# Converting DMAs on GpSimd's queue write the rounded part of the mixers' weight slabs

## The chip, the cores and the metric

One core of a Trainium2 chip runs the whole program. The metric is the device time of one execution in microseconds (us). The engines are TensorE (PE; its weight loads are listed as PEld), VectorE (DVE), ScalarE (ACT), GpSimd (POOL) and SyncE (SP); SyncE does nothing here but issue DMAs. TensorE's clock has two levels, 1.2 and 2.4 GHz; the granted clock is the share of the higher one that the profile recorded.

## The reference

One inference step of a small two-layer backbone, for 128 context tokens and 256 latent tokens with the same weights. D_MODEL is 1024, D_FF 2816. Each layer is a half-step feed-forward, a mixer and a second half-step feed-forward:

```python
h = rmsnorm(x, g[0]) * (1.0 + mod[:, 1]) + mod[:, 0]
x = x + 0.5 * mod[:, 2] * swiglu(h, p["w_ffn_in"][0], p["w_ffn_out"][0])
h = rmsnorm(x, g[1]) * (1.0 + mod[:, 4]) + mod[:, 3]
m, new_ctx = mixer(h, p, lidx, ctx)
x = x + mod[:, 5] * m
```

and the second feed-forward as the first. The factors mod come from a conditioning vector through w_ada (1024 x 9216 in each layer). In the mixer one projection w_in (1024 x 2144) feeds three groups of heads: differential attention (queries, keys and values, 256 columns each), a bidirectional gated recurrence of width 512 (input and gate branch, 512 columns each) and latent attention (352 columns). Their outputs are concatenated and go through w_out (1024 x 1024). Everything is float32.

## The kernel before

Activations stand with features on the 128 partitions and the 384 tokens along the free axis (context first). All 384 tokens go through one pass of the weights, and each weight is read from HBM once, in slabs: `wslab` (L460 to L472) loads up to four blocks of 128 input rows by 256 output columns (512 KB) into a tile wx with one or two DMAs on SyncE's queue.

To keep float32 accuracy from the faster float32r matmuls, both operands are split into a rounded part and a remainder. For a slab ScalarE casts wx into wh (float32r, L470), and VectorE writes wl = wx - wh (L471). `mm3` (L474 to L477) then runs three matmuls per pair of blocks: wh with the high part of the activations, wh with their low part, and wl with the high part. The tiles wh have four buffers (tag H), the tiles wl four (tag L), the tiles wx five (tag X); all slabs of the kernel, those of the feed-forwards too, go through these buffers.

There are 332 slabs. The mixer of a layer has 30: 18 of w_in (key "in": two each for the two halves of the recurrence's input, two each for the two halves of its gate branch, two for the values of the differential attention, four of 352 columns by two blocks for the latent attention, two each for queries and keys) and 12 of w_out (key "out"; for each pair of output blocks one slab of four blocks and two slabs of two). In the profile the mixer's matmuls write psw (recurrence), psva (values), psc (latent attention, 352 columns), psa (queries, keys) and po (out projection). The recurrence itself is gates (psg, L891), activations on ScalarE with several table loads, and scans on VectorE (L923, L924); after each scan GpSimd copies one column into state_out (L926), eight times per mixer in two groups of four. After psc, ScalarE squares it and writes the normalised cl (L143), which TensorE transposes (pst, L989).

The order of instructions on each engine is fixed when the program is built: the Tile framework reckons when each instruction is ready and gives the engine the ready one of highest priority. `ahead(key)` raises the priority of what stands in it; "in" has an offset of 120, "out" none. On each engine the instructions then run in that order, and one that waits holds all behind it.

GpSimd's queue carries the loads of w_ada in both layers (adax, L354, three buffers), small parameter loads (L226, L770), four stores of new context tensors per layer, and the copies into state_out. The ada steps run in the feed-forwards and, 14 of them, in the attention of layer 0's mixer.

Of the kernel before, what the change touches and what calls it, by code (L numbers as in the profile page):

```python
# [18 lines left out]
P = 128  # L19
# [65 lines left out]
def hybrid_step_kernel(  # L85
# [40 lines left out]
    nc = tc.nc  # L126
# [28 lines left out]
    def ahead(key):  # L155
        return tc.high_priority(offset=AHEAD[key]) if key in AHEAD else nullcontext()
# [303 lines left out]
    def wslab(pieces, nk, ncol, key):  # L460

        shape = [P, HALF_K, 256] if ncol <= 256 else [P, HALF_K // 2, 512]
        x = wp.tile(shape, F32, name="wx", tag="X")
        for src, off in pieces:
            n = src.shape[1]
            nc.sync.dma_start(x[:, 0:nk, off : off + n], src.rearrange("(k p) n -> p k n", p=P))
        h = wp.tile(shape, F32R, name="wh", tag="H", bufs=4)
        lo = wp.tile(shape, F32R, name="wl", tag="L", bufs=4)
        with ahead(key):
            nc.scalar.copy(h[:, 0:nk, 0:ncol], x[:, 0:nk, 0:ncol])  # L470
            V.tensor_tensor(lo[:, 0:nk, 0:ncol], x[:, 0:nk, 0:ncol], h[:, 0:nk, 0:ncol].bitcast(F32), ALU.subtract)  # L471
        return h, lo  # L472

# [81 lines left out]
    def ffn_slab(s, f, q):  # L555
        win = w_ffn_in[s // 3, (s % 3) // 2]
        rows = slice(q * HALF_K * P, (q + 1) * HALF_K * P)
        return wslab(
            [(win[rows, f * P : (f + 1) * P], 0), (win[rows, DFF + f * P : DFF + (f + 1) * P], P)], HALF_K, 256, "fin"
        )  # L560

    def ffn(s, r, hs, last, ready=None):
# [42 lines left out]
        for m in range(0, KD, 2):  # L605
            p2 = [PS("po0", "pw"), PS("po1", "pw")]
            parts = [(k0, min(HALF_K, KF - k0)) for k0 in range(0, KF, HALF_K)]
            if m == KD - 2:
                parts = parts[-1:] + parts[:-1]
            for n_, (k0, nk) in enumerate(parts):  # L610
                h, lo = wslab([(wout[k0 * P : (k0 + nk) * P, m * P : (m + 2) * P], 0)], nk, 256, "fout")
                n = ADA_F[s][1]
                ada.step(min(n, n * (slot + 1) // 16) - min(n, n * slot // 16), True)
                slot += 1
                for j in range(2):
                    for kk in range(nk):
                        w0 = slice(j * P, (j + 1) * P)
                        mm3(
                            p2[j][:, 0:T],
                            h[:, kk, w0],  # L620
                            lo[:, kk, w0],
                            *acts[k0 + kk],
                            n_ == 0 and kk == 0,
                            n_ == len(parts) - 1 and kk == nk - 1,
                        )
            if m == 0 and not last:
                ada.until(s + 1, 1)
            if m == KD - 4 and s % 3 == 0:
                ada.finish()
                cache_prep(l)  # L630
            for j in range(2):
                residual(p2[j], m + j, s, last)
                if last:
                    store_y(m + j)
# [182 lines left out]
    def mixer(l, r_in, hs):  # L817
# [8 lines left out]
        def in_slabs(cols):  # L826
            ncol = sum(b - a for a, b in cols)
            out = []
            for q in range(2):
                pieces, off = [], 0  # L830
                for a, b in cols:
                    pieces.append((W[rows(q), a:b], off))
                    off += b - a
                out.append(wslab(pieces, HALF_K, ncol, "in"))
            return out
# [558 lines left out]
```

## Time and profile before

| what | us |
|---|---|
| median of 3 runs (1579.6 to 1581.04) | 1579.62 |
| the profiled execution's own time | 1580.6 |
| its span, first to last instruction | 1578.8 |
| TensorE busy | 1527.9 |
| VectorE busy | 1113.6 |
| ScalarE busy | 746.6 |
| GpSimd busy | 103.4 |

The profiled execution has 1.8 us around its span, and it stands 1.0 us above the median. Busy times are unions of the instructions' intervals. TensorE's matmuls overlap in its pipeline, so busy time there is not speed. A wait is put down to the semaphore that came last. The mixer of layer 0 lies from about 327 to 523 us of the span, that of layer 1 from about 1096 to 1290 us. The granted clock over the span is 0.991.

### The profile page before, as it was taken

What the parts mean: (1) busy time and instruction counts of PE and PEld (TensorE: products, weight loads), DVE (VectorE), ACT (ScalarE), POOL (GpSimd) and SP (SyncE); (2) the same over time, 40 slices, a digit from 0 to 9 for tenths busy, and PEclk for the clock granted to TensorE, in tenths of its full rate; (3) what the DMA queues carried; (4) which work ended last, traced back from release to release, by engine and by line L of the source; (5) the groups of instructions that cost most, each with busy time, mean ns of one, the idle gap of its engine ahead of it and who ended that gap; (6) DMA issues with size and microseconds to landing.
All of it is one profiled execution on the core that took longest, in us unless ns stands there. A gap on an engine that the chain in (4) does not pass through costs nothing.

```text
span 1578.8 us, 24260 instructions
## 1 busy us (share of the span) xinstructions
PE 1527.9 (97%) x9118; PEld 1441.2 (91%) x9118; DVE 1113.6 (71%) x2068; ACT 746.6 (47%) x1376; POOL 103.4 (7%) x194
## 2 busy tenths in 40 slices
PE   7999999999889999999999999999978999999998
PEld 5899999998668999999999999999857699999998
DVE  5888586587677988578578866777967789443332
ACT  4533332469577633333363333325975864333221
POOL 1202010001100001001000200110000000000000
PEclk9999999999999999999999999999989999999999
DMA  9978576523531587566537866674231046444341
GB/s 304 248 205 228 158 231 196 147 80 115 185 106 37 146 245 211 161 207 225 171 97 215 238 187 193 203 238 121 64 92 37 15 134 201 130 117 128 116 145 35
DMA packets 291034, 249.02 MB, mean 158 GB/s; under 512 B 11554, under 2 KB 273159, under 8 KB 290917
## 3 DMA queue, kind: packets, MB, share of 16 engines
q1 hardware_dynamic: 270224, 175.94, 38.2%
q0 software_dynamic: 20368, 71.34, 14.8%
q8 instruction: 71, 1.16, 0.3%
q14 instruction: 47, 0.38, 0.1%
q10 hardware_dynamic: 324, 0.20, 0.1%
HBM read 245.17 MB, written 2.27 MB: 157 GB/s over the span
## 4 chain that ended last, share of the span: by engine, by line
PE 88%; DVE 4%; ACT 4%; issue 2%; DMA 1%; POOL 0%; ACTq 0%; DVEq 0%; POOLq 0%
PE po L475 9%; PE po L476 9%; PE po L477 9%; PE pg L475 8%; PE pg L477 8%; PE pg L476 8%; PE pu L475 8%; PE pu L477 8%; PE pu L476 8%; PE psw L476 1%; PE psg L891 1%; PE psw L475 1%; PE psw L477 1%; PE adaps L378 1%; ACT gate L143 1%
## 5 line engine op out<-in xcount | busy, mean ns | idle before, releaser
L471 DVE TENSOR_TENSOR wl<-wx,wh 128x1024 fp32r<-128x1024 f32 (+2 forms) x332 | 385.4, 1163 | 302.8 <-ACT wh L470 294.3
L470 ACT CAST wh<-wx 128x1024 fp32r<-128x1024 f32 (+2 forms) x332 | 333.2, 1005 | 448.5 <-PE po L476 237.3
L362 DVE SCALAR_TENSOR_TENSOR ada<-adax,sc,ada 128x1024 f32<-128x1024 f32 x196 | 244.2, 1280 | 17.8 <-DMA adax<-in_w_ada_dram 17.4
L475 PE MATMUL po<-aH,wh 128*128 128x384 f32 x704 | 239.7, 341 | 0.0
L477 PE MATMUL po<-aH,wl 128*128 128x384 f32 x704 | 237.7, 338 | 0.0
L476 PE MATMUL po<-aL,wh 128*128 128x384 f32 x704 | 237.2, 337 | 0.0
L475 PE MATMUL pg<-hH,wh 128*128 128x384 f32 x640 | 216.9, 339 | 0.0
L475 PE MATMUL pu<-hH,wh 128*128 128x384 f32 x640 | 216.2, 338 | 0.0
L477 PE MATMUL pg<-hH,wl 128*128 128x384 f32 x640 | 215.9, 337 | 0.2 <-DVE wl L471 0.2
L477 PE MATMUL pu<-hH,wl 128*128 128x384 f32 x640 | 215.6, 337 | 0.0
L476 PE MATMUL pu<-hL,wh 128*128 128x384 f32 x640 | 215.5, 337 | 0.0
L476 PE MATMUL pg<-hL,wh 128*128 128x384 f32 x640 | 215.4, 337 | 0.0
L143 ACT ACTIVATE sg<-pg 128x384 f32<-128x384 f32 x80 | 39.4, 493 | 206.5 <-PE pg L477 206.5
L475 PEld LDWEIGHTS po<-aH,wh 128*128 128x128 f32 x704 | 132.4, 188 | 3.9 <-issue 2.1
L476 PEld LDWEIGHTS po<-aL,wh 128*128 128x128 f32 x704 | 132.2, 188 | 0.5 <-issue 0.5
L477 PEld LDWEIGHTS po<-aH,wl 128*128 128x128 f32 x704 | 132.2, 188 | 0.0
L354 POOL DMA_DIRECT2D adax<-in_w_ada_dram x128 | 68.1, 533 | 892.3 <-DVE ada L360 466.5
L475 PEld LDWEIGHTS pg<-hH,wh 128*128 128x128 f32 x640 | 120.2, 188 | 2.5 <-issue 2.1
L477 PEld LDWEIGHTS pg<-hH,wl 128*128 128x128 f32 x640 | 120.1, 188 | 0.6 <-DVE wl L471 0.5
L476 PEld LDWEIGHTS pg<-hL,wh 128*128 128x128 f32 x640 | 120.2, 188 | 0.0
L475 PEld LDWEIGHTS pu<-hH,wh 128*128 128x128 f32 x640 | 120.2, 188 | 0.0
L477 PEld LDWEIGHTS pu<-hH,wl 128*128 128x128 f32 x640 | 120.1, 188 | 0.0
(327 smaller groups left out, 2425.9 us busy)
## 6 DMA issues: line engine op xcount, KB each, us to landing
wx<-in_w_ffn_in_dram SPq DMA_DIRECT2D x352, 256.0 KB, 4.1
adax<-in_w_ada_dram POOLq DMA_DIRECT2D x128, 512.0 KB, 4.9
wx<-in_w_ffn_out_dram SPq DMA_DIRECT2D x80, 512.0 KB, 3.9
wx<-in_w_in_dram SPq DMA_DIRECT2D x28, 512.0 KB, 3.8
adax<-in_w_ada_dram SPq DMA_DIRECT2D x16, 512.0 KB, 7.7
wx<-in_w_ffn_out_dram SPq DMA_DIRECT2D x16, 256.0 KB, 3.3
wx<-in_w_out_dram SPq DMA_DIRECT2D x8, 512.0 KB, 3.9
wx<-in_w_out_dram SPq DMA_DIRECT2D x16, 256.0 KB, 2.7
```

Source lines behind the costliest of these rows:

```text
L143: ins = nc.scalar.activation(out, in_, func, **kw)
L354: nc.gpsimd.dma_start(x, w_ada[l, k * P : (k + 1) * P, c0 : c0 + D])
L362: ins = V.scalar_tensor_tensor(accs[c], x, w, accs[c], ALU.mult, ALU.add)
L378: mm(bank[32 * a : 32 * a + 32, 256 * c : 256 * c + 256], cm(C_ONE, n1=32), x[:, a], start=True, stop=True)
L470: nc.scalar.copy(h[:, 0:nk, 0:ncol], x[:, 0:nk, 0:ncol])
L471: V.tensor_tensor(lo[:, 0:nk, 0:ncol], x[:, 0:nk, 0:ncol], h[:, 0:nk, 0:ncol].bitcast(F32), ALU.subtract)
L475: mm(out, wh, xh, start=first, stop=False)
L476: mm(out, wh, xl, start=False, stop=False)
L477: last_mm[0] = mm(out, wl, xh, start=False, stop=last)
L891: mm(ps[:, 0:TG], wg[:, wi, :], xcs[ch], start=True, stop=True)
```

## The change

In the slabs with key "in" or "out" the rounded part wh is no longer cast by ScalarE from wx. Instead the same pieces of the weight are read from HBM a second time, by DMAs on GpSimd's queue whose destination is the float32r tile wh; the transfer converts. wx is still loaded by SyncE, and VectorE still subtracts wh from wx. The feed-forwards' slabs are as before. The DMA stands outside `ahead(key)`.

```diff
         h = wp.tile(shape, F32R, name="wh", tag="H", bufs=4)
         lo = wp.tile(shape, F32R, name="wl", tag="L", bufs=4)
+        if key in ("in", "out"):
+
+            for src, off in pieces:
+                n = src.shape[1]
+                nc.gpsimd.dma_start(h[:, 0:nk, off : off + n], src.rearrange("(k p) n -> p k n", p=P))
         with ahead(key):
-            nc.scalar.copy(h[:, 0:nk, 0:ncol], x[:, 0:nk, 0:ncol])
+            if key not in ("in", "out"):
+                nc.scalar.copy(h[:, 0:nk, 0:ncol], x[:, 0:nk, 0:ncol])
             V.tensor_tensor(lo[:, 0:nk, 0:ncol], x[:, 0:nk, 0:ncol], h[:, 0:nk, 0:ncol].bitcast(F32), ALU.subtract)
```

## Rows read from the trace of the kernel before

**Rows 1.** The page: busy time, share of the span, instructions.

```profile
PE 1527.9 (97%) x9118; PEld 1441.2 (91%) x9118; DVE 1113.6 (71%) x2068; ACT 746.6 (47%) x1376; POOL 103.4 (7%) x194
```

**Rows 2.** Busy time by stage, both mixers; the sum covers all eight stages.

```profile
core 0: us, PE busy (x) PEld busy (x) DVE busy (x) ACT busy (x) POOL busy (x), PEclk, DMA share, GB/s
327.00:400.00 73.00, 71.67 (x423) 61.70 (x421) 62.68 (x141) 66.14 (x129) 7.04 (x14) 1.00 0.33 100
...
503.00:523.00 20.00, 20.00 (x116) 20.00 (x116) 18.45 (x50) 12.68 (x25) 0.00 (x0) 1.00 0.57 164
...
sum 390.00, PE 358.00 PEld 302.39 DVE 311.52 ACT 289.80 POOL 21.39; mean PE 44.75 PEld 37.80 DVE 38.94 ACT 36.23 POOL 2.67
```

**Rows 3.** TensorE's waits, 327 to 440 us: total, times, longest.

```profile
PE psva L955 <- DVE wl L471: 0.6, 1, 0.6
PE psc L981 <- DVE wl L471: 0.4, 1, 0.4
```

**Rows 4.** TensorE's waits, 1096 to 1210 us.

```profile
PE pst L989 <- ACT cl L143: 6.5, 1, 6.5
...
PE psc L979 <- ACT wh L470: 1.4, 1, 1.4
PE psc L981 <- DVE wl L471: 0.8, 1, 0.8
```

**Rows 5.** ScalarE's casts by shape, whole span: busy, mean ns of one.

```profile
L470 ACT CAST wh<-wx 128x1024 fp32r<-128x1024 f32 x292 | 307.3, 1053 | 381.8 <-PE po L476 176.5 <-PE pu L476 148.9 <-DMA wx<-in_w_ffn_in_dram 38.0
...
L470 ACT CAST wh<-wx 128x512 fp32r<-128x512 f32 x32 | 19.9, 622 | 66.2 <-PE po L476 60.8 <-PE psa L1212 2.8 <-ACT rH L143 1.5
...
L470 ACT CAST wh<-wx 128x704 fp32r<-128x704 f32 x8 | 6.0, 779 | 0.5 <-PE psw L476 0.5
```

**Rows 6.** DMA issues: count, KB each, median us from issue to landing.

```profile
wx<-in_w_in_dram SPq DMA_DIRECT2D x28, 512.0 KB, 3.8
...
wx<-in_w_ffn_out_dram SPq DMA_DIRECT2D x16, 256.0 KB, 3.3
...
wx<-in_w_out_dram SPq DMA_DIRECT2D x16, 256.0 KB, 2.7
...
wg<-in_lru_w_gate_dram POOLq DMA_DIRECT2D x4, 256.0 KB, 7.7
...
ukv<-in_mla_w_ukv_dram POOLq DMA_DIRECT2D x2, 256.0 KB, 4.3
```

**Rows 7.** GpSimd in order of time, 260 to 400 us: start, us, what.

```profile
366.78 0.48 POOL L926 COPY state_out<-hscan 128x1 f32<-128x1 f32 x1 [89.25 <-DVE hscan L923]
...
369.56 0.43 POOL L926 COPY state_out<-hscan 128x1 f32<-128x1 f32 x1 [0.40 <-DVE hscan L923]
372.59 0.56 POOL L926 COPY state_out<-hscan 128x1 f32<-128x1 f32 x1 [2.60 <-DVE hscan L923]
...
388.38 0.53 POOL L354 DMA_DIRECT2D adax<-in_w_ada_dram  x1
389.76 0.56 POOL L926 COPY state_out<-hscan 128x1 f32<-128x1 f32 x1 [0.85 <-DVE hscan L923]
```

**Rows 8.** VectorE, 365 to 374 us: the second va slab's subtraction.

```profile
370.98 1.22 DVE L471 TENSOR_TENSOR wl<-wx,wh 128x1024 fp32r<-128x1024 f32 x1
```

**Rows 9.** ScalarE, 1150 to 1180 us: a cast between the squares of psc.

```profile
1166.79 1.06 ACT L470 CAST wh<-wx 128x1024 fp32r<-128x1024 f32 x1
```

**Rows 10.** ScalarE, 318 to 332 us: a cast that waits for its buffer.

```profile
322.72 1.05 ACT L470 CAST wh<-wx 128x1024 fp32r<-128x1024 f32 x1 [3.14 <-PE po L476]
```

**Rows 11.** VectorE, 318 to 332 us: the last residual, then a subtraction.

```profile
327.13 0.74 DVE L547 SCALAR_TENSOR_TENSOR xT<-po,md,xT 128x128 f32<-128x128 f32 x2
328.02 1.23 DVE L471 TENSOR_TENSOR wl<-wx,wh 128x1024 fp32r<-128x1024 f32 x1 [0.16 <-ACT wh L470]
```

**Rows 12.** The ada loads on GpSimd: ns least, median, most.

```profile
L354 POOL DMA_DIRECT2D adax<-in_w_ada_dram x128: 530/530/657, 2.5 to 1333.6; - x128
```

## The prediction

> **What bounds the kernel now.** I read the page's busy times first. TensorE is busy for 97% of the span and ScalarE for 47% [rows 1], so taking work from ScalarE can only pay where TensorE waits for ScalarE. The change touches the two mixers alone, so next come the stretches of the two mixers, measured with the table by stage: 327 to 523 us in layer 0, 1096 to 1290 us in layer 1. TensorE is busy there for 358.0 of 390.0 us [rows 2]; the 32 us of idle time are all that any relief of another engine could give back. In the first part of layer 0's mixer (input projections and the recurrence) ScalarE is the fullest engine beside TensorE, 66.14 of 73 us, yet TensorE is busy 71.67 us of them: the projections fill it while the recurrence runs on ScalarE and VectorE.
>
> Then TensorE's waits, by what ended them. In layer 0 those that name a weight slab are 0.6 us (the remainder wl at the va projection) and 0.4 us (wl at the psc projection) [rows 3]. In layer 1 the row of 0.6 us at va comes again, and at psc they are 0.8 us and, for the rounded part wh itself, 1.4 us; the longest wait there is 6.5 us for cl, the normalised psc, which comes from ScalarE [rows 4]. So slabs cost 3.8 us in both mixers together, and a chain in which ScalarE's casts stand costs 6.5 us more.
>
> **What is removed.** Each mixer has 30 slabs: 14 of 512 KB and 4 of 352 KB of w_in, 4 of 512 KB and 8 of 256 KB of w_out. Their casts last 1.05, 0.78 and 0.62 us by shape [rows 5], so 2 x (18 x 1.05 + 4 x 0.78 + 8 x 0.62) = 54 us leave ScalarE. Most of it lies beside TensorE's work and gives nothing. What I count is the chain to cl in layer 1, where one cast of 1.06 us stands among the squares of psc [rows 9] and a second of the same kind follows before the normalisation: 2.1 us. VectorE's own subtractions hold the same chain, so I take 1.5 us a mixer, **-3.0 us**; bounds 0 and -4.2 us (2.1 in each).
>
> **What is added, and its latency.** 60 DMAs with 26.0 MB, on GpSimd's queue. No row shows a converting DMA, nor one of this shape on that queue. SyncE's load of the same 512 KB lands after 3.8 us, 256 KB after 2.7 [rows 6]. For 256 KB GpSimd's ukv takes 4.3 us where SyncE's w_ffn_out load takes 3.3, so the queue adds 1.0 us: I take 4.8 us for 512 KB, 3.7 for 256 and, between them by size, 4.1 for 352 KB. From below it can't beat SyncE's 3.8; from above it is wg, 256 KB in short pieces, at 7.7 us; the pieces here are 1 KB as in SyncE's load, so I stay near that. The Trainium skill ("DMA: Bandwidth & Descriptors", Latency and other measured facts) puts the first byte at about 1 us on GpSimd's path against 0.6 us on SyncE's, so 0.4 us more, not 1.0; by it the sum below would be 1.2 us lower, and no row here separates first byte from the rest.
>
> The bytes are costed at nothing: the DMA engines are busy 0.33 of the first part and none of the waits in [rows 3, 4] names a wx load; even in the out projection of layer 0, busy 0.57 at 164 GB/s [rows 2], some 2.3 MB more in 22 us (105 GB/s) make 0.57 x 269 / 164 = 0.93 of them. If that cover were gone, landings would move towards the 7.7 us bound.
>
> **The issue slot.** A DMA leaves when its instruction reaches the head of GpSimd's queue and an H buffer is free. GpSimd waits in order, and in each recurrence eight copies into state_out stand on it, each waiting for a scan on VectorE. The framework orders each queue by when it reckons instructions ready: loads of ada weights that come later in the source stand between these copies [rows 7]. I place the new DMAs where the present casts and subtractions imply that their buffer was reckoned free: the second va slab about the third copy, the third psc slab about the sixth.
>
> Second va slab: the third copy starts at 369.56; a cast of 1.05 us ahead of it on ScalarE's chain is gone; 368.5 + 4.8 to land + 1.22 to subtract = 374.6, against an end of 372.2 now (370.98 + 1.22, [rows 8]): TensorE 2.4 us later. Third psc slab: the sixth copy at 389.76, less four casts gone (3.6), plus the 2.4 just added, plus 4.1 to land and 0.9 to subtract = 393.5; the wait of 0.4 us there ends at 393.0 now. That is less late than TensorE itself then is, so it adds nothing, and the late arrival takes up waits of today: 2.4 - 0.4 in layer 0, 2.4 - 1.4 in layer 1, **+3.0 us**. Bounds: the DMAs leave ahead of the copies and the 3.8 us of waits go (-3.8); or behind the fourth copy, 372.59 + 4.8 + 1.2 = 378.6, 6.4 late in each mixer (+12.8).
>
> **The wait that moves.** Today ScalarE stands at a cast until TensorE frees the buffer (3.14 us at 322.72, [rows 10]). That wait goes to GpSimd, where only other DMAs and copies stand behind it; but VectorE's subtraction then waits for a landing. Queued behind it on VectorE are the residual and the norm of the mixer's start, which TensorE needs at once. The buffer free at 322.7 lands at 327.5 and is subtracted by 328.7; the residual of the last chunk starts today at 327.13 [rows 11]. It may be 1.6 us late; as the subtraction can also be placed behind it, I take 1 us a mixer, **+2.0 us**. Bounds 0 and, for the next slab (subtracted from 328.02 on, [rows 11], so free one cast earlier, at 327.0; 4.8 + 1.2 later is 333.0 against 329.2 now), 3.8 each, +7.6.
>
> **Out projections: nothing.** TensorE runs 116 matmuls in 20 us [rows 2], 0.172 us each. With four H buffers, 48 matmuls (8.3 us) lie between the freeing of one and the use of its next slab; 4.8 + 1.2, or 3.7 + 0.7, fit. At 7.7 + 1.2 the 512 KB slabs would be 0.6 us late, at most +2 us in all.
>
> **Sum.** -3.0 + 3.0 + 2.0 = +2.0 us on the profiled execution's own 1580.6 (span 1578.8 and 1.8 around it). The median of the runs is 1579.6, 1.0 below it, so I predict **1581.6 us**: no change that a measurement of this kernel tells, for which I count 0.2%, 3.2 us either way. Against the median, all lower bounds give 1579.6 - 4.2 - 3.8 = 1571.6, with all upper ones 1579.6 + 12.8 + 7.6 + 2.0 = 1602.0.
>
> **Rivals.**
> *GpSimd's queue becomes the wait (slower).* The va slab's DMA stands behind the fourth state copy: +12.8 - 3.0 + 2.0 = +11.8, 1591 us. For it: GpSimd stands 89 us at the first copy [rows 7], and the present casts of these slabs come only after the square roots that feed the scans. Against: ada loads do slip between copies. It decides from the point where the second va slab's DMA is issued later than about 370 us. Chance 0.22.
> *VectorE stands at the subtractions (slower).* Each mixer's start pays the 3.8 us: -3.0 + 3.0 + 7.6, 1587 us. For it: VectorE waits for casts there today. Against: it has idle time just there. Chance 0.13.
> *The DMAs run ahead (faster).* They are issued as buffers come free, before the copies: -3.8 - 3.0, 1573 us; a subtraction is then never late. For it: the first slabs of each mixer do have an empty GpSimd queue (277 to 366 us, the 89 us before the first copy). Against: the later slabs do not. Chance 0.25.
> *VectorE holds up the descriptors (slower).* If an issue on GpSimd lasted until a VectorE instruction of a subtraction's length is over, four late slabs would be 1.22 us later each, +4.9 on the sum, 1586.5 us. Against it: 128 issues of ada loads beside a busy VectorE lasted 530 ns in the median and 657 at most [rows 12]. Chance 0.04. The Trainium skill ("SBUF — State Buffer", SBUF: two separate sides) warns of this: GpSimd can't write descriptors while VectorE runs an operation on both of its ports. By that rule this is where the time would go; the trace so far doesn't show it.
>
> **How the numbers follow.** Forecast 0.36; faster 0.25; slower 0.22 + 0.13 + 0.04 = 0.39. The slower cases together are as likely as the forecast, but each alone is less so. The forecast's own range is 1576.4 to 1582.8. Eight in ten: down to the run-ahead case (1573), up to a little above the queue case, 1594, since a landing of 7.7 us would lift all of them.
>
> **What would show it.** Right: state copies and wh DMAs interleaved on GpSimd; landings near 4.8 us; TensorE's waits naming wl or a wh DMA at psva and psc some 2 us longer, the wait for cl shorter. Wrong: landings above 7 us; wh DMAs issued after the fourth or eighth copy; adax waits of TensorE in layer 0 longer; or no wait for a slab at all and both mixers shorter.

## The result: slower by 1.0%

The changed kernel takes 1594.6 us (median of 4 runs, 1590.8 to 1599.3) against 1579.6 us before: ratio 1.0099, 95% interval 1.0080 to 1.0117. That is 15.0 us slower, just above the range of the prediction, whose forecast was no change. The profiled execution has a span of 1593.4 us, 14.6 more than that of before.

**Where the time went.** I cut each mixer at TensorE's first matmuls: the norm (psn), the va projection (psva), the end of psc, the query and key projection (psa), the first out projection (po), the next norm. Lengths in us, layer 0 / layer 1:

| stage | before | after | difference |
|---|---|---|---|
| start: norm, recurrence's projections | 43.0 / 43.0 | 49.1 / 45.9 | +6.1 / +2.9 |
| va and psc | 28.3 / 28.3 | 26.3 / 26.2 | -2.0 / -2.1 |
| cl, latent queries and keys | 20.0 / 19.6 | 20.9 / 21.5 | +0.9 / +1.9 |
| queries and keys, up to the first out projection | 28.4 / 26.9 | 30.4 / 29.9 | +2.0 / +3.0 |
| attention and the rest | 76.7 / 76.3 | 77.9 / 79.1 | +1.2 / +2.8 |
| mixer | 196.4 / 194.1 | 204.6 / 202.6 | +8.2 / +8.5 |

So 16.7 us are lost in the mixers. Ahead of the first mixer 3.5 us were won, where the profile of before has 6.8 us at half clock (at 43 us) and that of after none; behind the mixers 1.4 us were lost. The page's busy line of the changed kernel, against [rows 1], shows ScalarE 48 us less busy without its 54 us of casts and GpSimd 43 us busier, with TensorE's busy time hardly changed:

```profile
PE 1530.3 (96%) x9118; PEld 1442.1 (91%) x9118; DVE 1114.9 (70%) x2068; ACT 698.3 (44%) x1316; POOL 146.7 (9%) x254
```

Windows by these stages after the change, first layer 0, then layer 1, and in the last three lines of before: layer 0's sum, layer 1's last stage and its sum (columns as in [rows 2]: length, then busy time of each engine, TensorE's granted clock, DMA share, GB/s):

```profile
323.40:372.50 49.10, 44.62 (x219) 39.35 (x218) 39.88 (x99) 31.19 (x63) 7.00 (x11) 0.97 0.60 150
...
398.80:419.70 20.90, 13.94 (x87) 6.86 (x87) 13.75 (x33) 7.92 (x26) 5.96 (x11) 0.84 0.87 268
...
sum 204.60, PE 185.01 PEld 152.97 DVE 157.88 ACT 123.89 POOL 34.61; mean PE 37.00 PEld 30.59 DVE 31.58 ACT 24.78 POOL 6.92
...
1172.80:1194.30 21.50, 11.32 (x31) 6.41 (x31) 14.70 (x35) 7.97 (x26) 1.86 (x3) 0.71 0.52 140
...
1224.20:1303.30 79.10, 75.27 (x442) 64.42 (x443) 60.76 (x196) 50.48 (x149) 6.26 (x9) 0.92 0.33 85
sum 202.60, PE 179.83 PEld 153.97 DVE 155.45 ACT 124.44 POOL 25.75; mean PE 35.97 PEld 30.79 DVE 31.09 ACT 24.89 POOL 5.15
...
sum 196.40, PE 183.86 PEld 152.99 DVE 157.15 ACT 144.64 POOL 15.06; mean PE 36.77 PEld 30.60 DVE 31.43 ACT 28.93 POOL 3.01
...
1213.70:1290.00 76.30, 71.30 (x442) 61.04 (x443) 62.49 (x198) 55.66 (x157) 0.54 (x1) 0.98 0.20 60
sum 194.10, PE 174.64 PEld 149.90 DVE 154.87 ACT 145.28 POOL 6.34; mean PE 34.93 PEld 29.98 DVE 30.97 ACT 29.06 POOL 1.27
```

In layer 0 TensorE idles 204.6 - 185.0 = 19.6 us, in the same stages of before 12.5. In layer 1 it idles 22.8 against 19.5, and is busy 179.8 us against 174.6 for the same matmuls: there the granted clock is 0.92 in the last stage, where it was 0.98 before. So of the 16.7 us 10.4 are idle time (7.1 and 3.3) and 6.3 longer busy time. Over both mixers the records show 37.5 us at the lower of the two levels, before 20.5. Most of these stretches begin in or right after a wait of 2 us or more; two of 3.4 us (at 1243 and 1267 us) have only waits under 1 us ahead of them.

**TensorE's waits**, layer 0 (323 to 440 us), then layer 1 (1100 to 1225 us), against [rows 3, 4]:

```profile
PE adaps L368 <- DMA adax<-in_w_ada_dram: 6.4, 2, 6.1
PE psn L503 <- ACT sq L143: 3.3, 1, 3.3
PE psw L481 <- DMA wh<-in_w_in_dram: 1.2, 1, 1.2
...
PE psva L961 <- DVE wl L477: 0.4, 1, 0.4
...
PE pst L995 <- ACT cl L143: 8.2, 1, 8.2
PE po L481 <- issue: 3.3, 1, 3.3
```

The waits for slabs at psva and psc are smaller than before, not larger. What grew is the wait for the norm at the start (nothing before, 3.3 us now), for cl (6.5 before), for the first out projection (2.2 before) and, in layer 0, for an ada load (6.1 now, 3.7 before). The ada row of before is not among [rows 3]:

```profile
PE adaps L368 <- DMA adax<-in_w_ada_dram: 4.8, 2, 3.7
```

The new DMAs themselves show why the first of these waits grew. By line, their durations of issue in ns (least, median, most) and who waited for them (us, times):

```profile
  L473 POOL DMA_DIRECT2D wh<-in_w_in_dram x36: 696/740/1000, 310.5 to 1172.9; - x36
  L473 POOL DMA_DIRECT2D wh<-in_w_out_dram x24: 696/707/775, 429.7 to 1293.1; - x24
...
who waited for it (us, times):
  DVE wl L477: 17.2, 13
  PE psw L481: 1.2, 1
```

TensorE waited for a landing once; VectorE waited 13 times, 17.2 us in all, at subtractions. On VectorE at layer 0's start (time, length, and in brackets the idle time before) one sees what stands behind such a wait, against [rows 11]:

```profile
319.42 1.23 DVE L477 TENSOR_TENSOR wl<-wx,wh 128x1024 fp32r<-128x1024 f32 x1 [1.02 <-DMA wh<-in_w_in_dram]
...
326.12 1.23 DVE L477 TENSOR_TENSOR wl<-wx,wh 128x1024 fp32r<-128x1024 f32 x1 [3.40 <-DMA wh<-in_w_in_dram]
327.26 0.74 DVE L553 SCALAR_TENSOR_TENSOR xT<-po,md,xT 128x128 f32<-128x128 f32 x2
```

The second of these two subtractions waited for a DMA that GpSimd issued at 319.47, when TensorE freed the buffer:

```profile
319.47 0.74 POOL L473 DMA_DIRECT2D wh<-in_w_in_dram  x1 [3.45 <-PE po L482]
```

The residual of the feed-forward's last chunk begins 3.9 us after TensorE's norm began at 323.4 (before, 0.2 us: 327.13 against 326.9). The norm's last squares need it, and TensorE stands 3.3 us for them. Between the queries' projection and their norm, in layer 0, the same:

```profile
431.51 1.07 DVE L1179 TENSOR_REDUCE nst<-sq 128x8 f32<-128x256 f32 x3 [0.47 <-ACT sq L143]
...
433.92 1.22 DVE L477 TENSOR_TENSOR wl<-wx,wh 128x1024 fp32r<-128x1024 f32 x1 [1.13 <-DMA wh<-in_w_out_dram]
435.07 0.17 DVE L662 TENSOR_TENSOR nst<-nst 128x24 f32<-128x24 f32 x1
436.01 0.69 DVE L477 TENSOR_TENSOR wl<-wx,wh 128x512 fp32r<-128x512 f32 x1 [0.77 <-issue]
...
437.04 1.08 DVE L1185 TENSOR_TENSOR ya<-psa,nst 128x256 f32<-128x256 f32 x3
```

From the first reduction to the normalised ya it takes 5.5 us; before it took 3.2:

```profile
430.49 1.07 DVE L1173 TENSOR_REDUCE nst<-sq 128x8 f32<-128x256 f32 x3
...
433.69 1.09 DVE L1179 TENSOR_TENSOR ya<-psa,nst 128x256 f32<-128x256 f32 x3
```

The two subtractions are of w_out slabs that TensorE uses from 450.1 us on. A third place of this kind lies at the end of each mixer: VectorE stands 1.3 us (layer 0) and 0.65 us (layer 1) for the landing of the last w_out slab, with work of the next norm behind it, and TensorE waits 0.8 and 1.3 us at that norm. Before, and with w_out cast by ScalarE (e1 below), there is no such wait.

### The profile page after: what moved, and what is told of

The parts are those of the page before. It is cut to its first block, busy times and chain, and to the rows that moved or that the text cites. A ratio compares the mean times of both kernels' runs of the same rounds, so it can differ in the third digit from the quotient of the medians.

```text
span 1593.4 us, 24305 instructions
## 1 busy us (share of the span) xinstructions
PE 1530.3 (96%) x9118; PEld 1442.1 (91%) x9118; DVE 1114.9 (70%) x2068; ACT 698.3 (44%) x1316; POOL 146.7 (9%) x254
## 4 chain that ended last, share of the span: by engine, by line
PE 78%; issue 9%; DVE 5%; DMA 3%; ACT 3%; POOL 1%; SPq 0%; POOLq 0%; DVEq 0%; ACTq 0%
PE po L481 8%; PE po L482 8%; PE po L483 8%; PE pg L481 8%; PE pg L483 8%; PE pu L483 8%; PE pu L481 8%; PE pu L482 8%; PE pg L482 8%; DMA adax<-in_w_ada_dram 1%; DVE wl L477 1%; DMA wh<-in_w_in_dram 1%; PE adaps L378 1%; PE psO L1112 1%; PE psT L1085 1%
## 5 line engine op out<-in xcount | busy, mean ns | idle before, releaser
L476 ACT CAST wh<-wx 128x1024 fp32r<-128x1024 f32 (+1 forms) x272 | 278.9, 1025 | 420.4 <-PE po L482 207.3
L482 PEld LDWEIGHTS pu<-hL,wh 128*128 128x128 f32 x640 | 120.3, 188 | 0.0
```

The costliest lines, as they stand in the source:

```text
L482: mm(out, wh, xl, start=False, stop=False)
```

## The experiments

Each was timed against the kernel before on the same chip; ratios are to that kernel, with 95% intervals. Expected times take 1594.6 and 1579.6 us as the two ends.

**1. Which slabs cost.** The change for some slabs only; the others are cast by ScalarE as before. "in_xb" to "in_qk" name the slabs of w_in by their use: the recurrence's input (the start), its gate branch, va, psc, and queries and keys.

```diff
-        if key in ("in", "out"):
+        if key in ("in",):                                              # e1
+        if key in ("in_gb", "in_va", "in_c", "in_qk", "out"):           # e2
+        if key in ("in_gb", "in_va", "in_c"):                           # e3
```

> Only the slabs of w_in (14 of 512 KB and 4 of 352 KB a mixer) come by the converting DMA; the 12 slabs of w_out a mixer are cast by ScalarE as before. Theory 'VectorE stands at landings': the loss sits where VectorE, which works in order, waits for a landing with critical work behind it: at the mixer's start (6.1 us lost in layer 0, 2.9 in layer 1) and between the key projection and the scores (about 3 and 5.5 us lost), where the first slabs of w_out are subtracted. Only the second loss can go here, up to 8 us of it: about 1587 us. Rival 'queue and bytes': the cost is of the 26.0 MB on GpSimd's queue, 8 MB of them are gone, so about a third of the 15 us: 1590 us. Rival 'the out projections cost nothing and win nothing': 1594.6 us as with the whole change.

> The first four slabs of each mixer (the xb projections) are cast by ScalarE as before; the other 26 slabs come by the converting DMA. Theory 'VectorE stands at landings': the 6.1 and 2.9 us lost between the last FFN chunk and the first projections come back, 1585.5 us. If only the two norms' waits of TensorE (4.1 and 2.3 us with the change) come back, 1589. Rival 'queue and bytes': 4 MB of 26.0 gone, 1592.5 us. Rival 'the loss at the start is taken up later anyway': 1594.6 us.

> The converting DMA is kept where slabs are needed while ScalarE is fullest and VectorE's waits hold up nothing that is late (the gelu, va and psc projections, 10 slabs a mixer); the xb, query, key and out slabs are cast by ScalarE as before. Theory 'VectorE stands at landings': the losses at the start and around the attention are gone and the gain of the psc stage (2.0 and 1.7 us in the changed kernel) stays: about 1576 us, faster than before. Rival 'queue and bytes': 9.1 MB of the 26.0 remain, a third of the loss: about 1584.5 us. Rival 'the psc gain is taken up by the next wait': 1579.6 us, no change.

Measured: w_in alone 1588.3 us, 1.0058 (1.0038 to 1.0077); the start cast 1586.9 us, 1.0040 (1.0028 to 1.0052); the middle slabs alone 1579.7 us, 0.9996 (0.9987 to 1.0005). So the start costs 7.7 us (1594.6 - 1586.9), the w_out slabs 6.3 (1594.6 - 1588.3), the middle nothing. By the ratios it is some 9 and 6 us, with intervals of about 4 us either way. The second run rules out its rival of queue and bytes (1592.5); the first can't tell its theory (1587) from that rival (1590). The third expectation, 1576, was missed, and its rival 'taken up by the next wait' had the right time. By stages the start takes 43.1 us in both layers when it is cast, and the queries' stage 28.2 and 27.3 us when w_out is cast. The middle slabs keep the -2.4 us of their stage in each mixer, and the time is still that of before. In that profile TensorE idles 29.3 us in the mixers, 2.7 less than before, but 30.7 us of them are at the lower clock, before 20.5, and the mixers are 1.1 us longer: this relief of ScalarE is worth nothing in the end.

**2. Bytes and queue without anyone who waits.** ScalarE casts, and each mixer slab is also read by a converting DMA into a scratch tile that nothing reads; in the second kernel each waits for the cast of its slab, and in the third the query and key slabs have none.

```diff
+            d = wp.tile(shape, mybir.dt.bfloat16, name="wd", tag="HD", bufs=1)
...
+                twin = nc.gpsimd.dma_start(d[:, 0:nk, off : off + n], src.rearrange("(k p) n -> p k n", p=P))
+                tc.add_manual_dep(twin.ins, cast.ins.name, sync, reason="after the cast")   # e8, e15
```

> ScalarE casts every slab as before, and for every slab of the mixers GpSimd's queue also issues a converting DMA of the same source bytes into a scratch tile that nothing reads (bfloat16, for room, so the bytes written are half). Theory 'VectorE stands at landings': nothing waits for those landings, so the time is that of before, 1579.6 us, at most 3 us more for ada loads behind them. Rival 'queue and bytes': the loss is there without anyone waiting for a landing, 1588 to 1594 us.

> As the kernel with ScalarE's casts and a second, unread converting DMA of every mixer slab, but now each such DMA waits for the cast of its slab, so that the 60 DMAs fall where the slabs are used and not at the start of the program (the scratch is one bfloat16 buffer, so a DMA also waits for the one before it). Theory 'VectorE stands at landings': the queue and the source bytes alone cost little, 1580 to 1583 us. Rival 'queue and bytes': most of the loss is here, 1588 us or more.

> ScalarE's casts and the unread second DMA behind each cast, for 26 of the 30 slabs of a mixer: all but the query and key slabs, whose DMAs stood in front of ada loads on GpSimd's queue in layer 0. Theory 'the queue and the bytes cost only where an ada load that is due stands behind a slab': the time of before, 1579 to 1581 us. Rival 'bytes cost by themselves': the 8.8 us of the run with all 30 shrink only in proportion, to 1587 us.

Measured: 1689.3 us, 1.069 (1.0663 to 1.0717); 1588.8 us, 1.0063 (1.0047 to 1.0078); 1582.2 us, 1.0018 (1.0008 to 1.0027). The first says nothing on the question: its DMAs wait for no buffer of the mixers, so they ran from the start of the program, each waiting for the one before it at the single scratch buffer, with ada loads behind them on GpSimd's queue. VectorE stood 121.2 us for ada loads in the first 340 us (8.0 before), with the feed-forward's subtractions behind it, and the last pg matmul of the first feed-forward began at 334 us instead of 226. The second has the time that its rival named (1588 us or more), but all of the loss lies in one place of layer 0 (cl's stage, 31.0 us instead of 20.0), where GpSimd stood at the single scratch buffer with ada loads behind it:

```profile
400.49 0.78 POOL L477 DMA_DIRECT2D wd<-in_w_in_dram  x1 [7.09 <-DMA wd<-in_w_in_dram]
401.26 0.55 POOL L354 DMA_DIRECT2D adax<-in_w_ada_dram  x1
409.06 0.74 POOL L477 DMA_DIRECT2D wd<-in_w_in_dram  x1 [7.25 <-DMA wd<-in_w_in_dram]
409.80 1.10 POOL L354 DMA_DIRECT2D adax<-in_w_ada_dram  x2
```

Layer 1 has no ada loads in its mixer, and all 30 extra DMAs. Of its five stages (43.0, 28.3, 19.5, 26.8 and 76.4 us) the first, the third and the sum:

```profile
1103.90:1146.90 43.00, 43.00 (x221) 38.23 (x220) 38.25 (x98) 37.87 (x71) 7.22 (x11) 1.00 0.59 112
...
1175.20:1194.70 19.50, 11.00 (x31) 6.31 (x31) 12.22 (x31) 9.03 (x23) 4.07 (x6) 0.74 0.70 126
...
sum 194.00, PE 174.61 PEld 149.94 DVE 154.92 ACT 145.01 POOL 27.12; mean PE 34.92 PEld 29.99 DVE 30.98 ACT 29.00 POOL 5.42
```

The five lengths are those of before to 0.1 us. With 26 of 30 slabs the loss is 2.6 us (1.3 to 4.3 by the interval), neither nothing nor the 7 us of the rival. So queue and bytes, as far as these kernels show them, cost some 3 us of the 15, where an ada load that is due stands behind a slab: TensorE's longest wait for one in layer 0 is 6.1 us after the change, 5.3 in this kernel, 3.7 before. (The scratch is written in half the bytes, and the third kernel leaves out the query and key slabs, so neither is fully tested.)

**3. The order on VectorE.** All 60 DMAs are kept; an edge without a semaphore puts a subtraction behind another VectorE instruction: e5, the start's third and fourth slab behind the norm's last small operation; e6, the first w_out slab behind the queries' stacked remainders and the next two behind the keys'; e7 both; e11 also the query and key slabs behind cl.

```diff
+            if after is not None:
+                behind(sub, after)
...
+        first = norm_last["newton"], norm_last["newton"]                                   # e5, e7, e11
+                sl = wslab([...], n, 256, "out", stk_last[min(nth[0], 1)] if nth[0] < 3 else None)   # e6, e7, e11
+            sl = in_slabs([(256 * kind, 256 * kind + 256)], (cl_last["dve"],) * 2)         # e11
```

> The whole change, with nothing but an order added on VectorE: the subtractions of the third and fourth slab of each mixer stand behind the norm's last small operation there (and so behind the residual and the squares it needs), instead of ahead of them. Theory 'VectorE stands at landings': the loss at the mixer's start is this order, so the time falls by what casting these slabs gave (1594.6 - 1586.9 = 7.7 us), to about 1587 us, with all 60 DMAs still there. Rival 'the landings are late for TensorE itself': the order changes nothing, 1594.6 us, and TensorE waits for the slabs instead.

> The whole change, with an order added on VectorE at the first three slabs of w_out of each mixer: the first slab's subtraction stands behind the last of the queries' stacked remainders, the next two behind the keys'. Theory 'VectorE stands at landings': the 5 us between the key projection and the scores in each mixer come from these subtractions standing in the chain of the queries' norm, so the time falls by what casting the w_out slabs gave (1594.6 - 1588.3 = 6.3 us), to about 1588 us. Rival 'the landings are late for TensorE itself' or 'queue and bytes': 1594.6 us.

> Both orders together, all 60 converting DMAs kept. Theory 'VectorE stands at landings': both losses go, 1594.6 - 7.7 - 6.3 = 1580.6 us, the time of before; with ScalarE freed of 54 us of casts still nothing is won beyond 2 us. Rival 'queue and bytes': about 1590 us or more.

> The whole change, all 60 converting DMAs, with three orders on VectorE: the start's third and fourth slab behind the norm, the query and key slabs behind cl, the first three slabs of w_out behind the stacked remainders. Theory 'subtractions that wait for landings in VectorE's chains, and PE's half-clock stretches that follow TensorE's idle time': the two orders alone gave 1589.4, the third takes 2 to 5 us of idle time at cl: 1583 to 1587 us. Rival 'what is left is of the queue' (ada loads behind the query and key slabs' DMAs in layer 0): 1588 to 1589.4 us.

Measured: 1592.6 us, 1.0086 (1.0071 to 1.0101); 1591.8 us, 1.0083 (1.0062 to 1.0104); 1589.4 us, 1.0065 (1.0049 to 1.0082); 1583.7 us, 1.0024 (1.0015 to 1.0033). The first three expectations were missed: each order alone gave 2 to 3 us, not 6 to 8, which is within the noise, and both together 5 us, not 14; 1589.4 us is close to what the rival 'queue and bytes' named. Only e11 came out as expected. Where it was put, the order did what it should. In e5 the start takes 45.2 and 43.8 us, so 6.0 of its 9.0 us are back; what is left in layer 0 is in part an ada step (16 matmuls, 1.7 us) that TensorE ran outside this stage before. But of the 6.6 us by which the mixers of that profile are shorter only 1.8 are left in the span: the stretch ahead of the first mixer is 2.6 us longer (3.4 us of it at half clock, none in the profile of the changed kernel), the stretches behind the mixers 2.1. In e6 the queries' chain takes 2.8 us (431.70 to 434.51), and that stage 28.0 and 28.2 us. In e7 the residual no longer waits, and the subtraction that held it comes 4 us later without a wait:

```profile
325.71 0.74 DVE L555 SCALAR_TENSOR_TENSOR xT<-po,md,xT 128x128 f32<-128x128 f32 x2
...
330.22 1.22 DVE L477 TENSOR_TENSOR wl<-wx,wh 128x1024 fp32r<-128x1024 f32 x1
```

TensorE has no wait of 0.2 us or more between 324 and 350 us there. But the time came back only in part until cl's chain was cleared as well: in the changed kernel four subtractions of 1.22 us, of query and key slabs, stand among cl's small operations, as they did before the change:

```profile
400.06 1.22 DVE L477 TENSOR_TENSOR wl<-wx,wh 128x1024 fp32r<-128x1024 f32 x1
401.19 0.29 DVE L723 TENSOR_SCALAR nst<-nst 128x3 f32<-128x3 f32 x1
...
402.27 2.58 DVE L477 TENSOR_TENSOR wl<-wx,wh 128x1024 fp32r<-128x1024 f32 x2
...
405.08 1.22 DVE L477 TENSOR_TENSOR wl<-wx,wh 128x1024 fp32r<-128x1024 f32 x1 [0.16 <-issue]
```

In e11 TensorE's wait for cl in layer 1 falls from 8.2 to 4.7 us.

**4. The same orders with fewer DMAs, and with none.** e9: DMAs for the middle slabs, order at cl; e10: no DMA, order at cl; e12: the start cast, all else by DMA, orders at cl and w_out; e18: as e12 without any DMA. In e9 and e10 the query and key casts stand behind cl too.

```diff
+        if key in ("in_gb", "in_va", "in_c"):                           # e9
+        if key in ("in_gb", "in_va", "in_c", "in_qk", "out"):           # e12
+        if key in ():                                                   # e10, e18
```

> The kernel with the converting DMA for the gelu, va and psc slabs alone, and with an order added: the four query and key slabs' casts and subtractions stand behind the last operations of cl, not among them. Theory 'the psc stage's gain waits at cl': cl's chain on VectorE holds four subtractions of 1.22 us, 4.9 us, that nobody needs for another 15 us; with them out, cl comes some 4 us earlier, the 2 us gained in the psc stage stay, and TensorE idles less: about 1573 us. Rival 'cl is held by the squares and the small operations': no change from 1579.7 us. Rival 'the ada loads decide in layer 0': only layer 1 gains, about 1576 us.

> The control: no converting DMA at all (the kernel before), with the same order at the query and key slabs. It tells what the order alone gives. Theory 'the psc stage's gain waits at cl': the wait of 6.5 us for cl in layer 1 shrinks by some 3 to 4 us, 1575 to 1576 us, 2 to 4 us above the same order with the DMAs of the middle slabs. Rival 'the DMAs of the middle slabs bring nothing even so': both kernels give the same time.

> The first four slabs of each mixer cast by ScalarE, all others by the converting DMA, with the orders at the query, key and w_out slabs. Theory 'VectorE's chains': the start costs nothing (1586.9 us without the orders), the w_out order gives some 4 us of the two mixers, the order at cl some 4 more: 1577 to 1580 us. Rival 'queue and bytes': no lower than 1584 us.

> The control without any converting DMA: every slab cast by ScalarE, with the orders at the query, key and w_out slabs as in the fastest kernel so far (1575.7 us). If the DMAs of 26 slabs bring something by themselves, this is slower by that, up to 1577.4 us (the control with the order at cl alone); if the orders are all, it is 1575 to 1576 us.

Measured: e9 1577.8 us, 0.9987 (0.9977 to 0.9997); e10 1577.4 us, 0.9987 (0.9978 to 0.9995); e12 1575.7 us, 0.9980 (0.9966 to 0.9994); e18 1573.9 us, 0.9967 (0.9953 to 0.9980). The order at cl is worth 2 us with the middle slabs' DMAs and without them: e9's 1573 us was missed, and e10's rival (the same time) was right. e12 and e18 came out below what was expected of them (1577 to 1580 and 1575 to 1577.4). The fastest median of all belongs to a kernel without converting DMAs; the intervals of e12 and e18 overlap, so the DMAs of 26 slabs bring nothing that can be measured. Against e18, which has two of the three orders and no DMA, the whole change with its three orders (e11) is 1.0024 / 0.9967, 0.6% or some 9 us slower. So the orders take about 6 us off what the change costs, and 9 remain.

**5. Which of the start's slabs.** e11 with two of the four cast by ScalarE: the first two (e16) or the next two (e17).

```diff
+            sl = in_slabs([...], (None, None) if half == 0 else first, "in" if half == 1 else "in_xb")   # e16
+            sl = in_slabs([...], (None, None) if half == 0 else first, "in" if half == 0 else "in_xb")   # e17
```

> The whole change with its three orders on VectorE, but the first and second slab of each mixer cast by ScalarE. Theory 'what is left at the start is the wait for the first two slabs' landings' (VectorE subtracts them ahead of the residual of the last FFN chunks): the 8 us between 1583.7 us (all slabs by DMA) and 1575.7 us (the start's four cast) are these two: 1576 to 1578 us. Rival 'the third and fourth slab': 1583 us, no change.

> The same, but the third and fourth slab of each mixer cast by ScalarE (their subtractions still behind the norm), the first two by the converting DMA. Theory 'the first two slabs': 1583 us, no change. Rival 'the third and fourth slab', whose DMAs are issued at the norm and whose landing the second half of the projection waits for: 1576 to 1578 us.

Measured: 1582.1 us, 1.0013 (1.0002 to 1.0024); 1580.1 us, 0.9998 (0.9988 to 1.0007). Neither theory: 1.6 us from the first two, which is within the noise, 3.6 from the next two, 8.0 from all four (e12).

**6. TensorE's clock.** 32 matmuls, whose result is overwritten, fill the wait for cl in layer 1, in the kernel after (e13) and in the one before (e14).

```diff
+            if l == 1 and t == 0:
+                for i in range(32):
+                    xh, xl = hs[i % KD]
+                    mm(ps[:, 0:T], xh[:, 0:P], xl, start=True, stop=True)
```

> The whole change, and in layer 1 TensorE runs 32 idle-time matmuls (128x384, their result is overwritten at once) between the last psc matmul and the transposes of cl, where it stands 8.2 us. Theory 'part of the loss is TensorE's clock, which falls after its waits': the half-clock stretch of 10.2 us there shortens, and the time falls by up to 5 us, to 1590 us, though 5 us of work is added. Rival 'the half-clock stretches cost nothing, since TensorE waits in them anyway': 1594 us as before.

> The control: the kernel before with the same 32 matmuls in layer 1, where TensorE stands 6.5 us for cl. Theory 'clock': its stretch of 10.2 us at half clock shortens too, 1575 to 1578 us. Rival 'costs nothing': 1579.8 us.

Measured: 1595.5 us, 1.0102 (1.0085 to 1.0119); 1578.7 us, 0.9993 (0.9983 to 1.0002). In e13 the wait fell from 8.2 to 2.5 us and the half-clock time of that stage from 12.3 to 6.2 us, and the stage is as long as without the fill (21.4 us, 21.5), for the fill itself takes 5.8. No time was won in either kernel. But the profile of e13, of the fastest of its six runs, gives a price of the clock further on. In the last stage of layer 1 TensorE runs the matmuls of the changed kernel at a granted clock of 1.00:

```profile
1224.00:1298.00 74.00, 69.71 (x443) 59.47 (x444) 60.29 (x196) 50.17 (x150) 6.25 (x9) 1.00 0.35 91
```

It is busy for 69.7 us there, and for 75.3 in the profile of the changed kernel, with 12.4 us at half clock: some 0.45 us for each. By this estimate the 17.0 us more at half clock in the mixers cost at most 7.7 us, less where TensorE stood waiting in them; the 6.3 us of longer busy time fit that. Why the clock fell in this stage in one run and not in the other isn't shown.

## Why the prediction was wrong

The sum failed in where a late landing is paid. It put +3.0 us on GpSimd's queue, where nothing was paid, +2.0 at the start, where casting the slabs gave back 7.7, nothing at w_out, where it was 6.3, and -3.0 for the casts, which brought nothing. By its own steps:

- *What is removed, -3.0.* It brought nothing. The casts went, but cl's chain holds four VectorE subtractions too, which I named ("VectorE's own subtractions hold the same chain") and then counted most of the relief all the same. In layer 0 TensorE's wait in that stage was for an ada load and not for cl, so there half of the term had no wait to shorten. cl's stage became 0.9 and 1.9 us longer; with the middle slabs alone by DMA the time is 0.9996 of before.
- *Latency.* Near: landings of 4.4 us for 512 KB of w_in (4.8 taken), 3.6 for 256 KB (3.7), 3.5 for 352 KB (4.1), against [rows 6]:

```profile
wx<-in_w_in_dram SPq DMA_DIRECT2D x28, 512.0 KB, 4.0
wh<-in_w_in_dram POOLq DMA_DIRECT2D x28, 512.0 KB, 4.4
...
wx<-in_w_out_dram SPq DMA_DIRECT2D x8, 512.0 KB, 5.0
...
wh<-in_w_out_dram POOLq DMA_DIRECT2D x8, 512.0 KB, 4.0
wh<-in_w_out_dram POOLq DMA_DIRECT2D x16, 256.0 KB, 3.6
...
wh<-in_w_in_dram POOLq DMA_DIRECT2D x8, 352.0 KB, 3.5
```

  Of the same 512 KB of w_in GpSimd's copy lands 0.4 us later than SyncE's, of the 256 KB of w_out 0.7 us later (3.6 against 2.9), of the 512 KB of w_out 1.0 us earlier. So my 1.0 us was not a constant of the queue, and SyncE's load no lower bound. The Trainium skill ("DMA: Bandwidth & Descriptors", Latency and other measured facts) has a difference of 0.4 us for the first byte; the w_in row agrees with it, the w_out rows do not.
- *The bytes: nothing.* Nearly right: some 3 us by experiment (e15), and TensorE's longest wait for an ada load in layer 0 went from 3.7 to 6.1 us.
- *The issue slot, +3.0.* It did not occur. The second va slab's DMA left at 365.03, ahead of the first state copy, and the third and fourth psc slabs ahead of the fifth, against [rows 7]:

```profile
365.03 0.74 POOL L473 DMA_DIRECT2D wh<-in_w_in_dram  x1 [8.89 <-PE psw L483]
369.24 0.48 POOL L932 COPY state_out<-hscan 128x1 f32<-128x1 f32 x1 [3.46 <-DVE hscan L929]
...
386.18 0.71 POOL L473 DMA_DIRECT2D wh<-in_w_in_dram  x1 [0.58 <-PE psva L961]
390.74 0.55 POOL L932 COPY state_out<-hscan 128x1 f32<-128x1 f32 x1 [3.85 <-DVE hscan L929]
```

  The waits of [rows 3, 4] for slabs mostly went, and the stage became 2 us shorter in each mixer: the lower bound was the truth here. I had inferred the order of GpSimd's queue from that of casts and subtractions.
- *The wait that moves, +2.0.* The mechanism was right, in its place and on its engine; the size was not: 9.0 us in the profile by stages (6.1 and 2.9), 7.7 us by experiment (e2). The upper bound, 7.6 us, is close to that, in part by luck: it is 3.8 us in each mixer, and in the profiles of e1, e6 and e13, with the same four DMAs at the start, the stage loses 5.3, 7.8 and 8.2 us in all. I had taken 1.0 of the 1.6 us of lateness because the subtraction "can also be placed behind" the residual; it was placed ahead, and it began 6.65 us after its slab's DMA was issued (319.47 to 326.12), not 4.8.
- *Out projections: nothing.* This step failed outright. I tested whether the slabs land in time for TensorE; they do, by 15 us (subtracted by 435.2, used from 450.1). I didn't ask what stands behind their subtractions on VectorE: the queries' norm, on which the whole attention waits. 6.3 us by experiment (e1), part of it at the norm behind the mixer.

Of the rivals, *VectorE stands at the subtractions* (0.13) named what the trace shows at the start and priced it at 7.6 us, but the sum kept +3.0 for the queue, which didn't come, and had nothing for w_out. *The DMAs run ahead* was right about the issue and wrong about its worth. *GpSimd's queue becomes the wait* is refuted by its own point of decision, 370 us. *VectorE holds up the descriptors*: 60 issues lasted 0.70 to 1.00 us, 0.74 and 0.71 in the median, beside a VectorE busy 70% of the span; nothing as long as a subtraction. The Trainium skill's warning ("SBUF — State Buffer", SBUF: two separate sides) is of VectorE operations that use both ports; the profile doesn't say which ran so here, and no issue shows a cost of that kind.

In all: 7.7 us at the start, 6.3 at w_out and about nothing in the middle make 14.0 of the 15.0 us, by leaving out parts. Through the order it is: 1594.6, 1589.4 with the two orders, 1583.7 with cl's, 1575.7 with the start cast. These don't add up to single causes: the orders at the start and at w_out alone gave 2 to 3 us each, and two orders took 5 to 6 us off the kernel before, without any DMA (e18). That the slabs of the start and of w_out cost the time is shown by leaving them out; that VectorE's order is the way they cost it is shown for the stages and for some 6 us, and argued for the rest. What stays open is the start under all three orders: casting its four slabs gives 8 us in the medians, though TensorE's recorded idle time in that stage of e11 is 0.1 and 0.7 us. The two profiles can't tell: their runs are 2.5 us apart (1582.0 and 1579.5), the start by 3.1 us, the ada step in layer 0 included, and the stretches behind the mixers by 1.7. Of the clock the runs show that it is the smaller part of the loss: at a mean granted clock of 0.992 the kernel before took 1577.4 to 1578.9 us and the changed kernel, in one run, 1590.8; at 0.988 and 0.989 it is 1579.8 to 1584.5 and 1593.6 to 1599.3.

## What to carry to other kernels

When a producer is replaced by a slower-landing one, ask for each consumer not only whether the data comes in time for the engine that needs the result, but what stands behind the consumer on its own engine, which runs in order; a transfer that is early for TensorE can still be late for VectorE's queue. An engine's relief counts only if nothing else holds the same chain: here moving four casts and four subtractions behind cl, with no other change, gave the 2 us that 54 us of removed casts did not. Before a producer is changed, try the order alone: the kernel before with two orders on VectorE has the fastest median of all, 0.3% below it.

## What I had not expected of the hardware

TensorE's granted clock fell to half in more places after the change (37.5 us instead of 20.5 in the mixers), for instance for 3.4 us from 328.6 us, right after the wait of 3.3 us for the norm, and in layer 1's mixer the same matmuls were 5.2 us longer busy. Runs of one kernel differ by 8.5 us with it: those of the changed kernel have a mean granted clock of 0.988 to 0.992, the fastest run the highest; those of e1 by 12.6, from 1581.8 us at 0.992 to 1594.4 at 0.985. And DMAs whose data nothing waits for held up the first feed-forward by 108 us, because loads that VectorE did wait for stood behind them on one queue (e4), while the 13 MB of layer 1, read in its mixer, cost nothing there (e8).
